# Two turned outputs into finished PSUM banks, and the last half's late sums, exponential and merge moved into block 7's first two quads

## The chip, the cores and the metric

The kernel runs on one core of one Trainium2 chip. The metric is the device time of one execution in microseconds (us). "A ratio" is fast runs of one kernel over fast runs of another, of the same rounds on the same chip. It is not quite the ratio of the medians quoted beside it.

Engines are named as in the profile: PE (the tensor engine, matmuls), DVE (VectorE), ACT (ScalarE), POOL (GpSimd). L382 is a line of the kernel.

## The reference

```python
def setup_inputs():
    m, k, n = 1024, 4096, 4096
    return {"a": randn(m, k), "b": randn(k, n)}      # float32

def reference(a, b):
    x = np.matmul(a, b)
    return special.logsumexp(x, axis=-1).astype(np.float32)
```

The 1024 x 4096 product is never stored. Its eight column blocks of 512 are reduced, one by one, to a maximum and a sum of exponentials per row, and these are merged at the end.

## The kernel before

The kernel computes most blocks with a two-by-two scheme of seven products (m1 to m7) instead of eight; VectorE makes the sums of operands that this needs (`t1`, `t3`, `t4`, `t6`, `t7`). It takes 16 matmuls for a product. Blocks 3 to 6 are "wide": each is done in two halves, whose outputs come out transposed. They are *turned* in 32 x 32 squares, and then reduced. Block 7 is done in four "quads" of seven products. After it come a reloaded block 0 and a reloaded block 1 for the last quarter of the rows.

How a wide half turns its four outputs and what it leaves for later:

```python
    def lse_turned(c, slot, h, r, by_rows=False):
        nm = tnm[:, 1 + h, ts(r, WN // 2)]
        v = blocks32(slot)
        nc.vector.transpose(out=slot, in_=c)
        nc.vector.tensor_reduce(out=nm, in_=v, axis=AX.X, op=ALU.max, negate=True)
        # ... (by_rows: 16 exponentials of 32 columns on ScalarE)
        add(v, v, nm.unsqueeze(-1).broadcast_to((P, WN // 2, 32)))
        nc.scalar.activation(out=slot, in_=slot, func=AF.Exp)
        return lambda: nc.vector.tensor_reduce(
            out=tts[:, 1 + h, ts(r, WN // 2)], in_=v, axis=AX.X, op=ALU.add
        )

    # end of wide_step; "last" is the last half before the narrow block 7
            end12 = lse_turned(c12, slots[0], 1, 0)
            end22 = lse_turned(c22, slots[1], 1, 1, True)
            product(c21, ...)                       # m4
            sub(s[:, 1], c21, s[:, 1])
            end12()
            end21 = lse_turned(c21, slots[0], 0, 1)
            end22()
            # t4, t7: all of them, or in the last half quarters 0 and 1
            product(c11, ...)                       # m7
            add(c11, c11, s[:, 1])
            e = fix_pool.tile([P, FD], f32, ..., tag="e")
            end11 = lse_turned(c11, e, 0, 0)
            end21()
            if last:
                # t4 and t7 of block 7, quarters 2 and 3: T4's upper half is where the slots lie
            deferred.extend([end11, merge_turned])
```

`deferred` runs in the next half or quad right after its first two sums; `pending` runs (by `flush`) just before these sums. `merge_turned` is a chain DVE, POOL, ACT, POOL on small tiles. The narrow quad, cut to the order of issue, which is each engine's order of execution:

```python
            m1(c11, start=True); m5(c12)
            nc.scalar.copy(out=e, in_=halves(r0))         # e = s[:, 0:2]
            m2(c21, start=True); m6(c22)
            nc.scalar.copy(out=s[:, 2], in_=c21)
            flush()
            if early and q == MP - 1:                     # block 7, fourth quad
                for g in range(G - 1):
                    last.make("t1", g * GI, (g + 1) * GI) # needs the load into aT
            add(s[:, 2], s[:, 2], e[:, 1])
            sub(s[:, 0], s[:, 2], e[:, 0])
            for f in deferred: f()
            # ... (more sums for the next blocks)
            m3(c12); nc.scalar.copy(out=x[:, 0], in_=c12) # x = s[:, 1::2]: over e[:, 1]
            m4(c21); nc.scalar.copy(out=x[:, 1], in_=c21)
            m7(c11)
            # ... (sums, then maxima; their exponentials go to pending)
            if early and q == 1:                          # block 7, second quad
                for what in ("t1", "t6", "t3"):
                    nxt.make(what)                        # 12 f16 sums on VectorE
            # ...
            if early and q == 1:
                spread_turned()                           # 32 small copies on GpSimd
                last = again1().load_all()                # 4 loads of b into aT, by GpSimd
```

## Time and profile before

| | before |
|---|---|
| median time | 421.74 us (421.0 to 422.65, 6 runs) |
| span of the profiled execution | 419.6 us |
| PE busy | 411.4 us, 98% |
| one wide half | 24.17 us |
| block 7's quads 1, 2, 3, 4 | 14.39, 12.22, 12.23, 12.23 us |
| reloaded block 0's quad | 12.22 us |

A quad's length is taken from the start of its first product to the start of the next one's. From the page: the first line gives each engine's busy time, share of the span and instructions, the second the clock that PE was granted, in tenths, in 40 slices of the span.

```profile
PE 411.4 (98%) x2747; PEld 260.9 (62%) x2747; DVE 316.5 (75%) x709; ACT 120.9 (29%) x447; POOL 92.0 (22%) x189
...
PEclk9999999999999999999999999999999999999999
```

So PE is the limit, and what can be won is the time in which it stands. The timeline of PE shows where (columns: start, duration, engine, line, operation, output and inputs, shape, count; in brackets the idle time before it and what ended it). The lines are the first quad's m1, m3, m4, m7, and the m1 of the second quad:

```profile
339.94 1.91 PE L554 MATMUL acc_0_0_3277<-tb,s_71 128*128 128x256 f16 x16
...
347.93 0.60 PE L554 MATMUL acc_0_0_3277<-b_0_2891,aT 128*128 128x256 f16 x4 [0.83 <-ACT s_0_3279 L621]
...
349.67 1.91 PE L554 MATMUL acc_0_1_3278<-tb,aT 128*128 128x256 f16 x16
352.58 0.60 PE L554 MATMUL acc_0_0_3277<-b_0_2891,aT 128*128 128x256 f16 x4 [1.00 <-ACT s_0_3279 L696]
...
354.33 1.91 PE L554 MATMUL acc_1_0_3411<-tb,s_71 128*128 128x256 f16 x16
```

The two brackets, 0.83 and 1.00 us by the profile's modelled ends, make a quad of 14.39 us instead of 12.22 (by the starts, against the second quad's, m3 came 1.0 us late and m7 2.16). In the timeline of ACT the copies that PE waited for (L621, L696) stand behind two exponentials that waited for others (L391 for c11 turned, L405 in the merge):

```profile
346.77 0.63 ACT L391 ACTIVATE ew_1_3259<-ew_1_3259 128x512 f32<-128x512 f32 x1 [3.01 <-DVE ew_1_3259 L86]
347.31 0.57 ACT L621 COPY s_0_3279<-acc_0_0_3277 128x512 f32<-128x512 f32 x1
...
351.99 0.28 ACT L405 ACTIVATE ident<-ident 128x96 f32<-128x96 f32 x1 [3.84 <-POOL ident L399]
352.18 0.35 ACT L696 COPY s_0_3279<-acc_0_0_3277 128x256 f32<-128x256 f32 x1
```

VectorE was late for the first; the merge, reached only when VectorE had done its sums, held up the second. GpSimd's timeline has the first and last of the 32 spread copies, which follow the merge, and the four loads into aT. The loads had to wait for the second quad's last product anyway:

```profile
353.94 0.19 POOL L415 COPY negmax<-ident 32x8 f32<-32x8 f32 x1
...
359.52 0.20 POOL L415 COPY tsum<-tts 32x8 f32<-32x8 f32 x1
366.00 3.56 POOL L149 DMA_DIRECT2D aT<-in_b_dram  x4 [6.28 <-PE acc_1_0_3411 L554]
```

### The profile page before, as it was taken

How to read it: one execution, taken by the hardware profiler on the slowest of the kernel's cores; microseconds unless marked ns; L12 is line 12 of the kernel's file. 1: busy time of each engine (PE TensorE's matmuls, PEld its weight loads, DVE VectorE, ACT ScalarE, POOL GpSimd, SP SyncE). 2: the span in 40 equal slices, each digit the busy share in tenths (PEclk: the TensorE clock that was granted, in tenths of full speed). 3: DMA queues.
4: the chain of work that ended last, by engine and by line, in shares of the span. 5: the costliest groups of instructions: out<-in, count | busy, mean ns of one | idle time of the engine just before them, and what ended most of it. 6: DMA issues, size and time to landing. Idle time of an engine off the chain costs nothing.

```text
span 419.6 us, 7085 instructions
## 1 busy us (share of the span) xinstructions
PE 411.4 (98%) x2747; PEld 260.9 (62%) x2747; DVE 316.5 (75%) x709; ACT 120.9 (29%) x447; POOL 92.0 (22%) x189
## 2 busy tenths in 40 slices
PE   8999999999999999999999999999999998999996
PEld 3555558888888844444444444444444477888885
DVE  2566587978656648969787896978789997299955
ACT  2222250141132210605134060514215052222124
POOL 8677743001010120013101031013100234320000
PEclk9999999999999999999999999999999999999999
DMA  9999999999999399004970099102990079499000
GB/s 186 201 202 203 203 205 207 207 207 214 178 200 185 54 186 207 9 2 75 207 121 0 2 165 207 29 1 35 207 160 2 0 120 207 76 186 208 10 2 0
DMA packets 57841, 53.28 MB, mean 127 GB/s; under 512 B 10192, under 2 KB 56912, under 8 KB 57808
## 3 DMA queue, kind: packets, MB, share of 16 engines
q0 software_dynamic: 48928, 49.95, 72.1%
q1 hardware_dynamic: 8880, 2.89, 4.3%
q8 instruction: 21, 0.34, 0.3%
q14 instruction: 12, 0.10, 0.1%
HBM read 100.66 MB, written 2.10 MB: 245 GB/s over the span
## 4 chain that ended last, share of the span: by engine, by line
PE 91%; DVE 4%; DMA 3%; issue 1%; ACT 0%; POOL 0%; SPq 0%; DVEq 0%; ACTq 0%; POOLq 0%
PE acc_1_0_1347 L554 2%; PE acc_1_0_767 L554 2%; PE acc_2_0_769 L554 2%; PE acc_2_0_3587 L554 2%; PE acc_0_0_765 L554 2%; PE acc_1_0_3411 L554 2%; PE acc_3_0_3723 L554 2%; PE acc_3_0_1615 L554 2%; PE acc_2_0_1482 L554 2%; PE acc_0_0_1215 L554 2%; PE acc_3_0_3859 L554 2%; PE wide_1_1_3085 L441 2%; PE wide_0_0_2899 L441 2%; PE wide_1_1_2707 L441 2%; PE wide_0_2_2523 L441 2%; PE wide_1_0_2328 L441 2%
## 5 line engine op out<-in xcount | busy, mean ns | idle before, releaser
L554 PEld LDWEIGHTS <-aT 128*128 128x128 f16 x832 | 81.3, 98 | 11.8 <-issue 2.2
L441 PEld LDWEIGHTS <-tb 128*128 128x128 f16 x384 | 37.6, 98 | 45.1
L382 ACT ACTIVATE tb<-tb,ident 128x32 f32<-128x32 f32 x128 | 39.1, 306 | 6.6 <-DVE ident L379 6.6
L391 ACT ACTIVATE tb<-tb 128x512 f32<-128x512 f32 x16 | 9.9, 622 | 89.6 <-DVE tb L86 89.6
L399 POOL TENSOR_TENSOR ident<-ident,tmin 128x96 f32<-128x96 f32 x8 | 3.1, 385 | 131.7 <-DVE tmin L401 131.7
L205 POOL DMA_DIRECT2D tb<-in_a_dram x47 | 25.6, 549 | 5.8 <-issue 1.9
L234 PEld LDWEIGHTS <-aT 128*128 128x128 f16 x192 | 16.6, 98 | 14.1 <-DVE aT L227 1.4
L229 ACT COPY aT<-tps_100 128x512 f16<-128x512 f16 x24 | 14.1, 586 | 38.5 <-PE tps_100 L216 38.5
L227 DVE COPY aT<-tps_99 128x512 f16<-128x512 f16 x24 | 10.2, 424 | 19.3 <-PE tps_99 L216 19.3
L382 ACT ACTIVATION_READ_ACCUMULATOR tb<-tb,ident 128x1 f32 x128 | 23.8, 186 | 0.0
L216 PEld LDWEIGHTS <-tb 128*128 128x128 f16 x192 | 14.8, 100 | 13.3 <-DMA tb<-in_a_dram 2.8
L554 PEld LDWEIGHTS <-s_71 128*128 128x128 f16 x208 | 20.4, 98 | 2.8
L554 PEld LDWEIGHTS <-s_73 128*128 128x128 f16 x208 | 20.4, 98 | 2.3
L554 PEld LDWEIGHTS <-s_72 128*128 128x128 f16 x208 | 20.4, 98 | 2.3
L379 DVE TENSOR_REDUCE ident<-tb 128x16 f32<-128x512 f32 x24 | 16.5, 686 | 1.4
L89 DVE TENSOR_TENSOR aT<-aT 128x256 f16<-128x256 f16 (+1 forms) x56 | 16.1, 339 | 0.0
L86 DVE TENSOR_TENSOR tb<-tb,ident 128x512 f32<-128x512 f32 x16 | 11.1, 692 | 0.6
L392 DVE TENSOR_REDUCE tts<-tb 128x16 f32<-128x512 f32 x16 | 10.8, 677 | 0.0
L216 PE MATMUL tps_99<-ident,tb 128*128 128x128 f16 x96 | 9.5, 223 | 0.6 <-DMA tb<-in_a_dram 0.4
L86 DVE TENSOR_TENSOR s_71<-aT 128x256 f16<-128x256 f16 (+1 forms) x26 | 8.1, 313 | 2.5 <-ACT aT L229 2.1
L216 PE MATMUL tps_100<-ident,tb 128*128 128x128 f16 x96 | 9.5, 222 | 0.0
L86 DVE TENSOR_TENSOR s_73<-aT 128x256 f16<-128x256 f16 (+1 forms) x26 | 8.1, 313 | 0.0
(907 smaller groups left out, 939.9 us busy)
## 6 DMA issues: line engine op xcount, KB each, us to landing
tb<-in_a_dram POOLq DMA_DIRECT2D x47, 128.0 KB, 5.9
aT<-in_b_dram POOLq DMA_DIRECT2D x4, 1024.0 KB, 15.1
b_1_86<-in_b_dram POOLq DMA_DIRECT2D x4, 256.0 KB, 6.4
b_2_87<-in_b_dram POOLq DMA_DIRECT2D x4, 256.0 KB, 6.2
b_3_88<-in_b_dram POOLq DMA_DIRECT2D x4, 256.0 KB, 6.2
b_0_89<-in_b_dram POOLq DMA_DIRECT2D x2, 512.0 KB, 9.3
b_1_90<-in_b_dram POOLq DMA_DIRECT2D x2, 512.0 KB, 12.5
b_2_91<-in_b_dram POOLq DMA_DIRECT2D x2, 512.0 KB, 15.9
```

The costliest lines, as they stand in the source:

```text
L86: nc.vector.tensor_tensor(out=o, in0=x, in1=y, op=ALU.add)
L89: nc.vector.tensor_tensor(out=o, in0=x, in1=y, op=ALU.subtract)
L205: nc.gpsimd.dma_start(out=slot, in_=a_m[m, :, k0 * P : (k0 + kn) * P])
L216: nc.tensor.matmul(pst[:, ts(j, P)], src[:, ts(j, P)], ident, is_transpose=True, start=(j == 0), stop=(j == kn - 1),)
L227: nc.vector.tensor_copy(out=dst, in_=v)
L229: nc.scalar.copy(out=dst, in_=v)
L234: nc.tensor.matmul(pt, aT[:, i, kp, m // 2, m % 2, :], blk0.raw[i // GI][:, i % GI, kp, :], start=(done[m] == 0), stop=(done[m] == KT - 1),)
L379: nc.vector.tensor_reduce(out=nm, in_=v, axis=AX.X, op=ALU.max, negate=True)
L382: nc.scalar.activation(out=v[:, i], in_=v[:, i], func=AF.Exp, bias=nm[:, i : i + 1], accum_out=tts[:, 1 + h, r * WN // 2 + i : r * WN // 2 ...
L392: return lambda: nc.vector.tensor_reduce(out=tts[:, 1 + h, ts(r, WN // 2)], in_=v, axis=AX.X, op=ALU.add)
L441: nc.tensor.matmul(c.rearrange("p (q m) -> p q m", m=P), lhs(i), rhs(i), start=(start and i == 0), stop=(stop and i == KP - 1), skip_group ...
L554: nc.tensor.matmul(c, lhs(i), rhs(i), start=(start and i == 0), stop=(i == KP - 1), skip_group_check=True,)
```

## The change

The intent: turn c21 into c22's PSUM bank and c11 into c12's, products that are finished and turned by then. The slots, which lie in T4's upper half, are then free earlier. In the last half, the late T4 and T7 sums, c21's sum and c11's exponential go behind the first quad's copies and sums; c11's sum and the merge go on to the second quad (through `pending`).

```diff
-            end21 = lse_turned(c21, slots[0], 0, 1)
+            end21 = lse_turned(c21, c22, 0, 1)
...
-            e = fix_pool.tile([P, FD], f32, name=f"ew_{blk.nb}_{nt}", tag="e")
-            end11 = lse_turned(c11, e, 0, 0)
-            end21()
+            exp11, end11 = lse_turned(c11, c12, 0, 0, late=True)
             if last:
                 for what in ("t4", "t7"):
                     for g in range(G // 2, G):
-                        mk(what, g * GI, (g + 1) * GI)
-            deferred.extend([end11, merge_turned])
+                        deferred.append(lambda w=what, g=g: nxt.make(w, g * GI, (g + 1) * GI))
+                deferred.extend([end21, exp11])
+                deferred.append(lambda: pending.extend([end11, merge_turned]))
+            else:
+                exp11()
+                deferred.extend([end21, end11, merge_turned])
```

(`lse_turned` returns the exponential and the sum apart when `late` is set.)

More of the change, by code (lines that the diff above doesn't have):

```diff
@@ L373, with lse_turned @@
     blocks32 = lambda t: t.rearrange("p (c n) -> p c n", n=32)
-    def lse_turned(c, slot, h, r, by_rows=False):
+    def lse_turned(c, slot, h, r, by_rows=False, late=False):
         nm = tnm[:, 1 + h, ts(r, WN // 2)]
@@ L390, in lse_turned @@
         add(v, v, nm.unsqueeze(-1).broadcast_to((P, WN // 2, 32)))
-        nc.scalar.activation(out=slot, in_=slot, func=AF.Exp)
-        return lambda: nc.vector.tensor_reduce(
+        exp = lambda: nc.scalar.activation(out=slot, in_=slot, func=AF.Exp)
+        total = lambda: nc.vector.tensor_reduce(
             out=tts[:, 1 + h, ts(r, WN // 2)], in_=v, axis=AX.X, op=ALU.add
         )
+        if late:
+            return exp, total
+        exp()
+        return total
     def merge_turned():
```

## The prediction

> **What bounds the kernel.** The tensor engine: by the page 411.4 of 419.6 us busy at full granted clock, and 91% of the chain of waits. In the timeline the wide halves follow each other every 24.17 us with no PE gap, and the quads after block 7's first take 12.2 us each. After the start-up (62 us, which the change leaves alone) there is one hole: block 7's first quad runs from 339.94 to 354.33 us, 14.39 against 12.22. So 2.17 us (0.5%) is all the change can win.
>
> **Why the hole is there** (timeline, chain). VectorE is late; it idles 0.4 us between 327 and 351 us. The last wide half ends on it with c11's add, turn, reduce, add (until 346.66), then c21's sum, four late makes of T4 and T7 (347.37 to 349.78), and only then the quad's two sums, c11's sum and the merge. ScalarE, in order, holds back the quad's copies twice:
> - c11's exponential waits 3.0 us for VectorE until 346.77, so the copy of c11|c12 starts at 347.31 and m3 about 1 us late (347.93);
> - the merge's exponential waits 3.84 us until 351.99, so the copy of m3's result starts at 352.18 and m7 about 1.2 us late (352.58).
>
> **What the change does.** It removes no work: the same VectorE operations of 0.6 to 0.75 us and exponentials of 0.62 us, two outputs turned into PSUM instead of SBUF. That empties the slots, which share T4's upper half, so the late makes need not wait for c21's sum. In the last half the late makes, c21's sum and c11's exponential move behind the quad's copies and sums; c11's sum and the merge move into the second quad.
>
> The Trainium skill ("Perfetto Trace Analysis", Optimizing Scalar/DVE Operations) puts VectorE's access overhead at about 60 ns on SBUF, 125 ns on PSUM. The trace shows no such difference: maxima read from PSUM take 0.68 us and follow every 0.60, like reductions in SBUF. My estimate is 0 to 0.5 us per half, inside the 4 us that VectorE idles (20.2 busy of 24.2).
>
> **The quad re-timed**, with the second quad's offsets: first copy at 343.8 us; m2/m6's copy 347.1; VectorE sums 347.5 to 348.3; makes at 348.3, 348.9, 349.5, 350.1, done 350.8. m3 starts on time at 346.95; m4 at 348.70, needing T4's third quarter at 349.57 (ready 349.0) and fourth at 350.0 (349.6); m7 at 350.45, needing its last quarter at 351.75 (350.8). c11's exponential fits in at 347.5. All waits vanish, with 0.4 to 0.5 us of slack; the second quad starts near 352.2.
>
> **Given back later?** The merge's exponential now sits behind the second quad's copy (about 359.6), so GpSimd's spread and the load into aT go out near 367 us instead of 366.0, with the PE 2.2 us ahead. The last quarter's sums then wait some 3 us on VectorE, which idles 4 us before the final quad. I expect no PE loss.
>
> **Predicted:** 421.74 - 2.1 = 419.6 us, 8 in 10 within 418.8 to 420.9. Faster by over 2%: 0.005; within 2%: 0.985; slower: 0.01.
>
> **Would show it right:** no PE wait on ScalarE in block 7's first quad, its length near 12.2; wide halves still 24.17; VectorE durations on PSUM unchanged; the aT load about 1 us later; the tail unchanged.
>
> **Would make it wrong:** slower PSUM targets, making VectorE late for m4 or m7; m4 waiting for all of T4 instead of quarters (about 1 us lost); the later load reaching the final quads.

## More of the kernel before

Note for later: the copy into `x[:, 0]` overwrites `e[:, 1]`, so it has to wait until VectorE has read it; m7 waits for that copy; and the tile `s` has one buffer, shared by all quads.

One more place matters later, the fourth quad. In VectorE's timeline the three T1 sums that need the load (tb from aT) stand ahead of the quad's first sum (s_3_3725):

```profile
383.77 1.89 DVE L86 TENSOR_TENSOR tb<-aT 128x1024 f16<-128x1024 f16 x3
386.37 0.43 DVE L86 TENSOR_TENSOR s_3_3725<-s_3_3725 128x256 f32<-128x256 f32 x1 [0.72 <-ACT s_3_3725 L625]
```

Here that sum waits for ACT, by 0.72 us, and not for the load.

## The result, and the profile after

| | before | after |
|---|---|---|
| median time | 421.68 us (20 runs) | 425.84 us (425.58 to 426.42, 10 runs) |
| ratio | | 1.0102 (95%: 1.0091 to 1.0112) |
| span of the profiled execution | 419.6 us | 423.1 us |
| block 7's quads 1, 2, 3, 4 | 14.39, 12.22, 12.23, 12.23 | 12.23, 12.23, 12.22, 18.09 us |
| reloaded block 0's quad | 12.22 | 12.22 us |
| loads into aT issued, before the fourth quad's start | 12.78 us | 5.58 us |

The kernel became 1% slower. The 2.16 us of the first quad were won exactly as forecast, and 5.86 us were lost in the fourth. The page:

```profile
PE 411.8 (97%) x2747; PEld 260.9 (62%) x2747; DVE 315.6 (75%) x709; ACT 120.5 (28%) x447; POOL 96.2 (23%) x189
...
PEclk9999999999999999999999999999999999999899
```

PE's timeline, first quad (m1, m3, m4, m7, and the next m1, cut off after 11 of its 16 matmuls by the end of the window asked for): no bracket is left.

```profile
339.65 1.91 PE L560 MATMUL acc_0_0_3263<-tb,s_71 128*128 128x256 f16 x16
...
346.64 0.60 PE L560 MATMUL acc_0_0_3263<-b_0_2884,aT 128*128 128x256 f16 x4
...
348.38 1.91 PE L560 MATMUL acc_0_1_3264<-tb,aT 128*128 128x256 f16 x16
350.13 0.60 PE L560 MATMUL acc_0_0_3263<-b_0_2884,aT 128*128 128x256 f16 x4
...
351.88 1.36 PE L560 MATMUL acc_1_0_3395<-tb,s_71 128*128 128x256 f16 x11
```

PE's timeline, the fourth quad's m7 (the first and last of four groups of four matmuls; then the next quad's m1):

```profile
391.28 1.01 PE L560 MATMUL acc_3_0_3715<-b_0_2884,aT 128*128 128x256 f16 x4 [4.30 <-ACT s_3_3717 L702]
...
393.80 0.79 PE L560 MATMUL acc_3_0_3715<-b_3_2887,aT 128*128 128x256 f16 x4
394.42 1.91 PE L560 MATMUL acc_3_0_3851<-s_71 128*128 128x256 f16 x16
```

m7 should have begun 10.48 us after its quad, as in the first quad, at 386.81. It began at 391.28, 4.47 us late; and its 16 matmuls then took 3.14 us (391.28 to 394.42) instead of 1.75, which is 1.39 us more. Together that is the 5.86 us. The bracket names ACT's copy into x (L702). ACT in turn had waited for VectorE. Its timeline, the merge's exponential and this copy:

```profile
359.06 0.37 ACT L631 COPY s_1_3397<-acc_1_1_3396 128x256 f32<-128x256 f32 x1 [2.86 <-PE acc_1_1_3396 L560]
359.33 0.29 ACT L409 ACTIVATE ident<-ident 128x96 f32<-128x96 f32 x1
...
390.86 0.37 ACT L702 COPY s_3_3717<-acc_3_0_3715 128x256 f32<-128x256 f32 x1 [5.62 <-DVE s_3_3717 L86]
```

And VectorE had waited for the load: three T1 sums, then the quad's first sum that the copy needs.

```profile
381.33 0.68 DVE L86 TENSOR_TENSOR tb<-aT 128x1024 f16<-128x1024 f16 x1
384.71 0.69 DVE L86 TENSOR_TENSOR tb<-aT 128x1024 f16<-128x1024 f16 x1 [2.70 <-DMA aT<-in_b_dram]
389.74 0.69 DVE L86 TENSOR_TENSOR tb<-aT 128x1024 f16<-128x1024 f16 x1 [4.34 <-DMA aT<-in_b_dram]
390.35 0.42 DVE L86 TENSOR_TENSOR s_3_3717<-s_3_3717 128x256 f32<-128x256 f32 x1
```

GpSimd's timeline says why the load was late: the merge's second step waited 4.61 us for ACT, whose exponential stood behind a copy of the second quad; then the 32 copies, of which the first take 0.19 us (but for one of 0.69) and the last eight some 0.6; and then the loads, with no wait of their own.

```profile
359.70 0.44 POOL L403 TENSOR_TENSOR tts<-tts,ident 128x96 f32<-128x96 f32 x1 [4.61 <-ACT ident L409]
...
361.08 0.19 POOL L419 COPY negmax<-ident 32x8 f32<-32x8 f32 x1
...
365.69 0.19 POOL L419 COPY tsum<-tts 32x8 f32<-32x8 f32 x1
365.93 0.65 POOL L419 COPY negmax<-ident 32x8 f32<-32x8 f32 x1
366.52 0.66 POOL L419 COPY tsum<-tts 32x8 f32<-32x8 f32 x1
...
370.14 0.67 POOL L419 COPY tsum<-tts 32x8 f32<-32x8 f32 x1
370.75 3.57 POOL L149 DMA_DIRECT2D aT<-in_b_dram  x4
```

The granted clock in the stretch of m7, with the busy time of the engines (the columns are named by the first line):

```profile
core 0: us, PE busy (x) PEld busy (x) DVE busy (x) ACT busy (x) POOL busy (x), PEclk, DMA share, GB/s
391.20:394.50 3.30, 3.22 (x17) 2.29 (x17) 1.83 (x4) 0.30 (x2) 0.00 (x0) 0.55 0.84 142
```

### The profile page after: what moved, and what is told of

It reads as the page before. It is cut to its first block, busy times and chain, and to the rows that moved or that the text cites. A ratio compares the mean times of both kernels' runs of the same rounds, so it can differ in the third digit from the quotient of the medians.

```text
span 423.1 us, 7100 instructions
## 1 busy us (share of the span) xinstructions
PE 411.8 (97%) x2747; PEld 260.9 (62%) x2747; DVE 315.6 (75%) x709; ACT 120.5 (28%) x447; POOL 96.2 (23%) x189
## 4 chain that ended last, share of the span: by engine, by line
PE 86%; DMA 8%; POOL 3%; issue 1%; DVE 0%; ACT 0%; POOLq 0%; ACTq 0%; DVEq 0%
DMA aT<-in_b_dram 4%; DMA tb<-in_a_dram 3%; PE acc_1_0_1347 L560 2%; PE acc_1_0_767 L560 2%; PE acc_2_0_769 L560 2%; PE acc_3_0_3851 L560 2%; PE acc_0_0_3263 L560 2%; PE acc_3_0_1615 L560 2%; PE acc_2_0_1482 L560 2%; PE acc_0_0_1215 L560 2%; PE acc_0_0_765 L560 2%; PE wide_1_2_3078 L445 2%; PE wide_0_0_2892 L445 2%; PE wide_1_1_2701 L445 2%; PE wide_0_2_2518 L445 2%; PE wide_1_0_2324 L445 2%
## 5 line engine op out<-in xcount | busy, mean ns | idle before, releaser
L391 ACT ACTIVATE tb<-tb 128x512 f32<-128x512 f32 x8 | 5.0, 630 | 90.1 <-DVE tb L86 90.1
L379 DVE TENSOR_REDUCE ident<-tb 128x16 f32<-128x512 f32 x16 | 11.0, 686 | 1.1
L86 DVE TENSOR_TENSOR tb<-aT 128x1024 f16<-128x1024 f16 x8 | 5.2, 687 | 8.7 <-DMA aT<-in_b_dram 8.7
L86 DVE TENSOR_TENSOR s_71<-aT 128x256 f16<-128x256 f16 (+1 forms) x26 | 8.2, 314 | 2.4 <-ACT aT L229 1.5
L86 DVE TENSOR_TENSOR s_72<-aT 128x256 f16<-128x256 f16 (+1 forms) x26 | 8.2, 314 | 0.0
L86 DVE TENSOR_TENSOR s_73<-aT 128x256 f16<-128x256 f16 (+1 forms) x26 | 8.1, 313 | 0.0
```

The source lines that it names most:

```text
L86: nc.vector.tensor_tensor(out=o, in0=x, in1=y, op=ALU.add)
L391: exp = lambda: nc.scalar.activation(out=slot, in_=slot, func=AF.Exp)
```

## The experiments

My theory after the result: the merge and the spread delay the load into aT; VectorE's order then turns the late load into a wait of PE; and the wait brings a slow clock. The rivals: the PSUM targets cost the time; or the load is late for a reason of its own; or only the order of VectorE's work is at fault, not the lateness. The profile already spoke against the first (wide halves of 24.17 us, the same turning times), but only an experiment can say what each part costs by itself. All experiments but one gave a correct result.

| run | chip | this, us | before, us | ratio (95%) | load's lead, us | quads 1, 4, next |
|---|---|---|---|---|---|---|
| e1 loads first | 5 | 419.54 | 421.46 | 0.9952 (0.9940 to 0.9964) | 12.78 | 12.23, 12.23, 12.22 |
| e2 before, loads first | 5 | 421.52 | 421.46 | 0.9999 (0.9987 to 1.0011) | 12.78 | 14.40, 12.22, 12.23 |
| e3 merge after quad 1 | 5 | 419.39 | 421.46 | 0.9946 (0.9934 to 0.9958) | 12.78 | 12.23, 12.23, 12.22 |
| e4 sums first | 5 | 424.63 | 421.46 | 1.0094 (1.0070 to 1.0118) | 5.58 | 12.23, 12.23, 17.45 |
| e5 PSUM only | 1 | 421.22 | 421.24 | 1.0004 (0.9992 to 1.0016) | 12.78 | 14.18, 12.23, 12.22 |
| e6 late, SBUF, loads first | 1 | 419.39 | 421.24 | 0.9961 (0.9949 to 0.9973) | 12.78 | 12.64, 12.23, 12.22 |
| e7 filler | 1 | 424.67 | 421.24 | 1.0088 (1.0075 to 1.0102) | 5.59 | 12.23, 16.66, 12.98 |
| e8 no sums (wrong result) | 1 | 421.00 | 421.24 | 1.0007 (0.9986 to 1.0029) | 9.03 | 12.22, 13.26, 12.99 |
| e9 24 copies first | 12 | 420.02 | 421.54 | 0.9957 (0.9941 to 0.9972) | 10.51 | 12.23, 12.23, 12.62 |
| e10 both mends | 12 | 419.28 | 421.54 | 0.9942 (0.9928 to 0.9956) | 12.78 | 12.23, 12.22, 12.23 |
| e11 after again | 14 | 425.83 | 421.48 | 1.0103 (1.0086 to 1.0119) | 5.58 | 12.23, 18.01, 12.66 |

"Lead" is the start of the fourth quad less the start of the first load's issue; "next" is the reloaded block 0's quad.

### e1: the loads ahead of the spread

```diff
             if early and q == 1:
-                spread_turned()
                 last = again1().load_all()
+                spread_turned()
```

> The changed kernel with the four loads into aT put ahead of the 32 spread copies on GpSimd. Theory (the load goes out 4.8 us late because it stands behind the copies): load issued at about 364 us, when the second quad's last product ends, no wait in block 7's fourth quad (12.2 us instead of 18.1), no slow clock after it; 419.5 us, 2.2 below the kernel before. The 32 copies now run under VectorE's f16 sums and take about 0.6 us each, harmless. Rival (the PSUM targets or the moved VectorE work cost the time, and the load only shows it): stays near 425.8.

Measured: 419.54 us. The loads went out at 363.54 us, the fourth quad took 12.23 us, and PE's only waits are in the start-up. GpSimd's timeline, the loads and the first of the copies behind them:

```profile
363.54 3.57 POOL L149 DMA_DIRECT2D aT<-in_b_dram  x4 [2.54 <-PE acc L560]
367.07 0.70 POOL L419 COPY negmax<-ident 32x8 f32<-32x8 f32 x1
```

The whole loss came from the load's place behind the copies. The rival that PSUM or the moved VectorE work costs the time is out. The copies behind the load are as slow as expected, and harm nothing, since only the last merge reads what they write.

### e2: the same swap in the kernel before

```diff
             if early and q == 1:
-                spread_turned()
                 last = again1().load_all()
+                spread_turned()
```

> The kernel before with the same swap (loads ahead of the spread). There GpSimd already waited 6.3 us for the second quad's products before the load, so the load cannot go out earlier than 366.0: theory says same, 421.7 within 0.3. If the swap is a gain by itself, 419 to 421.

Measured: 421.52 us, ratio 0.9999. The swap is no gain by itself; it only takes away what the change brought in.

### e3: the merge at the end of the first quad

```diff
-                deferred.append(lambda: pending.extend([end11, merge_turned]))
+                deferred.append(lambda: after_quad.extend([end11, merge_turned]))
...
                 maxima()
+            for f in after_quad:
+                f()
+            after_quad.clear()
```

> The changed kernel with c11's sum and the merge issued at the end of block 7's first quad, ahead of the second quad's copies on ScalarE, and the load still behind the spread. Theory (the merge's exponential stood 4.6 us behind a copy, which pushed the spread under VectorE's f16 sums): merge's exponential near 355.1, copies of 0.19 us done by about 362.5, load issued near 364.0, fourth quad 12.2 us; 419.5 us. Rival (the spread is slow or late whatever the merge does): fourth quad still over 15 us, 423 or more.

Measured: 419.39 us. GpSimd's merge step now waits 0.40 us for ACT, where it waited 4.61, and the loads go out at 364.16 with all the copies done before, at 0.19 us for most and 0.29 at most:

```profile
356.11 0.38 POOL L404 TENSOR_TENSOR tts<-tts,ident 128x96 f32<-128x96 f32 x1 [0.40 <-ACT ident L410]
...
357.37 0.19 POOL L420 COPY negmax<-ident 32x8 f32<-32x8 f32 x1
...
364.16 3.57 POOL L149 DMA_DIRECT2D aT<-in_b_dram  x4 [0.78 <-PE acc L561]
```

So the merge's place on ACT is the root. Late by 4.6 us, it pushed the last copies under VectorE's sums, and these pushed the load.

### e4: the fourth quad's sums ahead of the load-dependent ones

```diff
-            if early and q == MP - 1:
-                for g in range(G - 1):
-                    last.make("t1", g * GI, (g + 1) * GI)
             add(s[:, 2], s[:, 2], e[:, 1])
             sub(s[:, 0], s[:, 2], e[:, 0])
+            if early and q == MP - 1:
+                for g in range(G - 1):
+                    last.make("t1", g * GI, (g + 1) * GI)
```

> The changed kernel with the fourth quad's two sums put ahead of the three T1 sums that wait for the load. Theory (the load's lateness itself costs, since VectorE's work that depends on it has to be done before the next quad's sums): the wait leaves the fourth quad, but one of 3 to 5 us on ScalarE's copy comes in the next quad (the reloaded block 0), since its sums stand behind eight f16 sums that now start near 396 us; 423.5 to 426.5. Rival (only the order of these sums behind the load-dependent ones costs, VectorE has slack to absorb the rest): no wait anywhere, 419.5.

Measured: 424.63 us. The fourth quad took 12.23 us, and the next one 17.45. ACT's timeline has its first copy, PE's the m3 that waited for it:

```profile
397.95 0.59 ACT L627 COPY s<-acc 128x512 f32<-128x512 f32 x1 [10.14 <-DVE acc L86]
```

```profile
398.58 3.02 PE L560 MATMUL acc<-b,aT 128*128 128x256 f16 x16 [2.45 <-ACT s L627]
401.39 2.51 PE L560 MATMUL acc<-s,aT 128*128 128x256 f16 x16
404.68 1.91 PE L560 MATMUL acc<-b,aT 128*128 128x256 f16 x16 [0.78 <-ACT s L702]
```

Total as expected, place as expected, cause of the larger wait not: I had named the next quad's sums. The copy into `e` waited 10.14 us for VectorE's adds into the fourth quad's outputs, which come behind the load-dependent sums. It fits that the tile `s` has one buffer, so that the next quad cannot fill it before the last one's readers are done. The sums that I had named account for the smaller wait, 0.78 us before m7. The rest of this quad's loss is the clock: m3 took 2.81 us instead of 1.75, and the granted clock was at half from 399.2 to 402.6 us. The order on VectorE decides where the late load hurts; it does not remove the loss.

### e5: PSUM targets alone

```diff
-            end21 = lse_turned(c21, slots[0], 0, 1)
+            end21 = lse_turned(c21, c22, 0, 1)
...
-            e = fix_pool.tile([P, FD], f32, name=f"ew_{blk.nb}_{nt}", tag="e")
-            end11 = lse_turned(c11, e, 0, 0)
+            end11 = lse_turned(c11, c12, 0, 0)
```

> The kernel before with only the two targets of the turning moved into PSUM (c21 into c22, c11 into c12), no order changed. Theory (PSUM targets cost and bring nothing by themselves): 421.7 within 0.4, hole of the first quad still 2.2 us, wide halves 24.17 us, turning and sums 0.6 to 0.75 us each as on SBUF. Rival (PSUM targets are slower on VectorE by tens of ns per operation): VectorE later by 0.2 to 0.5 us at the end of the last half, hole longer by as much, 422 or more.

Measured: 421.22 us, ratio 1.0004: neither cost nor gain that these runs can tell. The first quad's hole is still there, 14.18 us against 14.39.

### e6: the moved order with SBUF targets

```diff
-            end21 = lse_turned(c21, c22, 0, 1)
+            end21 = lse_turned(c21, slots[0], 0, 1)
...
-            exp11, end11 = lse_turned(c11, c12, 0, 0, late=True)
+            e = fix_pool.tile([P, FD], f32, name=f"ew_{blk.nb}_{nt}", tag="e")
+            exp11, end11 = lse_turned(c11, e, 0, 0, late=True)
             if last:
+                deferred.append(end21)
...
-                deferred.extend([end21, exp11])
+                deferred.extend([exp11])
```

(and the loads ahead of the spread, as in e1)

> The changed kernel with the loads ahead of the spread and both outputs turned into SBUF as before; c21's sum must then come before the late makes, 0.6 us later for T4's third quarter (near 349.6 us, with m4 needing it at about 349.6). Theory (the moved order closes the hole, PSUM only frees the slots so that the makes need not wait): first quad 12.2 to 12.8 us; 419.5 to 420.1. If the PSUM targets carry the gain: the hole stays near 2 us, 421.5.

Measured: 419.39 us, ratio 0.9961, within the noise of e1's 0.9952. The first quad took 12.64 us instead of 12.23; its m4 (349.46 to m7's start at 351.61) took 2.15 us instead of 1.75. So the moved order closes the hole, and the PSUM targets add the last 0.4 us by the trace; the times cannot tell them apart.

### e7: filler in the wait

```diff
+            if early and q == MP - 1:
+                dummy = psum_pool.tile([P, FD], f32, name="dummy", tag="ps")[:, 0:H]
+                for i in range(36):
+                    nc.tensor.matmul(dummy, s1[:, i % KP, q], aT[:, i % KP, 0, q], start=True, stop=True)
             m7(c11)
```

> The changed kernel with 36 idle-filling products (128 x 256, results unused) ahead of the fourth quad's last product, where the tensor engine waits some 4.3 us. Theory (16 products after the wait took 3.30 us instead of 1.75 because the engine had stood idle): the wait shrinks to about 0.4 us, the 16 products take 1.75 us, the time falls by 1.5 us to about 424.3; the load is as late as before. Rival (the products are slow because of what VectorE or the transfers do at that time): still 3.3 us, 425.8 or more.

PE's timeline: the filler, the shortened wait, m7, and the next m1.

```profile
386.88 4.09 PE L708 MATMUL dummy<-aT,s 128*128 128x256 f16 x36
391.31 1.91 PE L560 MATMUL acc<-b,aT 128*128 128x256 f16 x16 [0.34 <-ACT s L702]
393.06 1.91 PE L560 MATMUL acc<-s 128*128 128x256 f16 x16
```

m7 took 1.75 us again (391.31 to 393.06), with VectorE and the transfers as late as before (m7 4.43 us behind its place). The granted clock, asked in windows of 0.1 us, stayed at 1.00 through both quads. The slow matmuls were thus due to PE standing idle, and 1.39 us of the fourth quad's loss were the clock. The time fell by less than the expected 1.5 us, since the next quad, starting earlier, now met the late VectorE and took 12.98 us instead of 12.22. The net over the two quads is 0.67 us. The ratio went from 1.0102 to 1.0088, but the two intervals overlap, so the gain in time is shown by the trace alone.

### e8: the changed kernel without the twelve sums (wrong on purpose)

```diff
-            if early and q == 1:
-                for what in ("t1", "t6", "t3"):
-                    nxt.make(what)
```

> The changed kernel without the twelve f16 sums that VectorE makes for the reloaded block 0 after the second quad (result wrong on purpose). Theory (the spread copies on GpSimd take 0.6 instead of 0.19 us because VectorE's f16 sums run at the same time): all 32 copies near 0.19 us, load issued near 367 us instead of 370.8, wait in the fourth quad 0 to 1 us, 419.5 to 420.5. Rival (late copies because of the merge's late exponential alone, copies slow for another cause): eight copies still 0.6 us, load after 370, 425 or more.

The last copies on GpSimd now take 0.20 us, and the load goes out 9.03 us before the fourth quad instead of 5.58:

```profile
368.09 0.20 POOL L419 COPY tsum<-tts 32x8 f32<-32x8 f32 x1
368.23 3.57 POOL L149 DMA_DIRECT2D aT<-in_b_dram  x4
```

The late copies are slow because VectorE's sums run beside them: that accounts for 9.03 - 5.58 = 3.45 us of the 7.20 us by which the load's lead shrank, and the merge's place for the other 3.75. One of the 32 copies still took 0.70 us, as in the changed kernel; there it began at 363.01, when a VectorE subtraction (two SBUF inputs) had begun at 362.96. The fourth quad lost 1.03 us and the next 0.77. The time, 421.00 us, is above the expected 419.5 to 420.5, because I had left out the loss in the next quad.

### e9: 24 copies, then the loads, then eight copies

```diff
             if early and q == 1:
-                spread_turned()
+                spread_turned(range(3))
                 last = again1().load_all()
+                spread_turned(range(3, 4))
```

(`spread_turned` takes the groups as an argument.)

> The changed kernel with 24 of the 32 spread copies ahead of the loads into aT and the eight that ran slowly behind them. Theory (the loss is set by how long before the fourth quad the load goes out: 5.6 us in the changed kernel gave 4.5 us of wait in it, 9.0 us without the twelve sums gave 1.0 there and 0.8 in the next): load issued near 366 us, 10.4 us before the fourth quad; no loss in the fourth quad, 0.2 to 0.6 us in the next; 419.5 to 420.1, at most 0.6 above the version with all copies behind. Rival (any load behind the merge loses time): 421 or more.

Measured: 420.02 us; a lead of 10.51 us, no loss in the fourth quad, 0.40 us in the next. With e8 and the changed kernel this gives three points of loss against lead: 10.51 us costs 0.40, 9.03 costs 1.80, 5.58 costs 5.86 with the slow clock. For the fourth quad one number fits all three. In the changed kernel the lead shrank by 7.20 us and m7 came 4.47 late, so 2.73 us were to spare. In e8 it shrank by 3.75, which leaves 1.02, and the quad lost 1.03; in e9 by 2.27, which leaves nothing, and nothing was lost. So e8's missing sums did not distort its point there; for the next quad that was not tested.

### e10: both mends

The edits of e1 and e3 together.

> The changed kernel with both mends: merge at the end of the first quad, loads ahead of the spread. The load waits for the second quad's last product in either, so theory: no gain over one mend alone, 419.4 within 0.4. If a second hidden cost remained in one of them: below 419.

Measured: 419.28 us, ratio 0.9942. No gain over one mend alone that these runs can tell. It has the lowest median of the versions, though not by more than the noise, and it is the simplest one to defend, since neither the merge nor the spread is then in the load's way. Each of e1, e3, e6, e9 and e10 beats both kernels.

### e11: the changed kernel again

> The changed kernel once more, unedited: its first profile explains 3.4 us of loss, while the runs showed 4.2 and the profiled run was its fastest. Theory (the wait for the load varies between executions, since it follows transfers): a second profile shows the same two changes, the first quad 12.2 us and the fourth between 17.5 and 19.5, all other quads 12.2 us; median 425 to 426. Rival (a further loss elsewhere that the first profile did not have): another quad or a wide half longer by 0.5 us or more.

Measured: 425.83 us, ratio 1.0103. The second profile has the same two changes, and the fourth quad's wait is as long (m7 4.56 us behind its place). But the slow matmuls now reached into the next quad, which took 12.66 us; here m7 and that quad's m1:

```profile
393.18 3.19 PE L560 MATMUL acc<-b,aT 128*128 128x256 f16 x16 [4.39 <-ACT s L702]
396.15 2.34 PE L560 MATMUL acc<-s 128*128 128x256 f16 x16
```

No other quad is longer by 0.5 us. Over the two quads the loss was 6.22 us against 5.86 in the first profile. The theory's reason did not show itself: the wait was the same within 0.1 us. What varied is where the slow clock lay. Asked in windows of 0.1 us, the granted clock is at half for 3.41 us in both profiles (and in e4), but from 390.75 us in the first, 0.53 before m7 began, and from 393.61 in this one, 0.43 after m7 began, so that more of it fell on work.

This does not explain why the usual loss (4.2 us, by the medians) is 0.7 us above that of the profiled spans (423.1 - 419.6 = 3.5 us): of the ten runs behind the median, nine have the mean clock of the first profile or 0.001 above it (0.994, 0.995), and only one has this one's 0.991. Some 0.3 us of it may be that block 7 began at 339.65 us in the first profile after and at 339.94 in the one before; the rest stays open (block 7 began anywhere from 339.3 to 341.5 us in the profiles of all runs, so the start-up alone moves single runs by more than that).

## Why the prediction was wrong

1. **The hole in the first quad.** Right: 14.39 us became 12.23, all the waits went, and the second quad began 12.23 us after the first. The offsets from the quad's start were right within 0.1 us (m3, m4 and m7 on time), but for the first copy, which waited for c11's sum on VectorE and came 0.7 us later than forecast (344.23); that cost nothing. With the loss taken away (e1, e3, e10) the median is 419.3 to 419.5 us, where the forecast said 419.6.
2. **PSUM as a target.** Right: e5 is the same as before. Turning into PSUM takes 0.72 to 0.73 us against 0.72 into SBUF, the sum in place 0.70 against 0.69.
3. **"I expect no PE loss."** This is the step that failed; it lost 5.86 us. The prediction had named "the later load reaching the final quads" as a thing that would make it wrong, but put no loss on it. The step had two mis-sized terms and one thing overlooked:
   - *The load near 367 us, about 1 us later than before.* It went out at 370.75, 4.75 us later. I saw the merge's exponential go behind the second quad's copy (forecast 359.6, measured 359.33), but took the 32 copies at the 0.19 us that they had in the profile before. There VectorE was idle or reading PSUM. Moved later, the last eight ran beside VectorE's f16 sums at 0.56 to 0.67 us. The Trainium skill has this in "SBUF — State Buffer", section "SBUF: two separate sides": VectorE and GpSimd share a pair of ports, by an exclusive lock for a whole instruction, and a VectorE operation with two SBUF inputs takes it against a GpSimd operation that reads SBUF. The trace agrees, and e8 shows it by experiment: without the sums the copies take 0.20 us.
   - *"The last quarter's sums then wait some 3 us on VectorE."* I looked only at the last quarter of the load. The first three quarters' T1 sums stand ahead of the fourth quad's own sums on VectorE; the copy into x needs these, and m7 needs the copy. That path had 2.73 us to spare (e9), and the load came 7.20 us nearer. Nor would the forecast time of the load have been harmless: e8's lead of 9.03 us, which is about a load at 367.3 on the changed kernel's clock (376.33 - 9.03), still cost 1.80 us. VectorE's 4 idle us before the final quad come too late to help: PE has lost its time by then.
   - *The clock.* I had no term for it. PE stood for 4.3 us, and the next 16 matmuls took 3.14 us instead of 1.75. The Trainium skill's "TensorE: Matmul & The Clock Gate" ("What's actually happening") says that PE falls to half its clock after an idle window of about 3.4 us. The trace agrees (the granted clock was 0.50 from 390.75 to 394.16 us, after a wait of 4.3 us; for a shorter wait see the last section), and e7, by filling the wait, took away the 1.39 us.
4. **The sum.** Predicted -2.1 + 0; measured -2.16 + 4.47 + 1.39 = +3.70 in the quads of the first profile, with the median of the runs at +4.2. The mechanism of the gain was right and of the right size; the term "given back later" was put at 0 and was 5.86.

Ruled out: a cost of PSUM (e5, to within 0.2%), a gain of the swapped loads as such (e2), and a fault of order alone (e4).

## What to carry to other kernels

When work is moved behind a later point on one engine, follow it on to the engines that it feeds until the next transfer is issued: here a merge put behind one copy brought the last of 32 tiny copies under VectorE's sums, and a load 7.2 us nearer to its use. Take a duration over only if its neighbours stay the same; here a GpSimd copy took 0.19 us beside an idle VectorE and about 0.6 beside its sums. And issue a load ahead of any work in its queue that nobody waits for.

## What the Trainium skill lacked or had wrong

- "TensorE: Matmul & The Clock Gate" ("What's actually happening") names an idle window of about 3.4 us before the clock falls. In e4 a shorter wait did it: by the bracket 2.45 us, by the start 2.61 us late, and the 16 matmuls after it took 2.81 us (398.58 to 401.39) instead of 1.75. The granted clock fell at 399.20 us, when PE had already been at work again for 0.62 us. Waits of 1.0 us by the bracket (first quad of the kernel before) did not do it.
- "SBUF — State Buffer" ("SBUF: two separate sides") has the lock but no figure for many small GpSimd operations beside a row of VectorE sums. Here a 32 x 8 copy of 0.19 us took 0.56 to 0.67 us beside f16 sums that repeat every 0.60, so that each copy cost about one sum. That is no rule: in e9 the first copy behind the loads took 4.11 us (370.07 to 374.18), about as long as the rest of VectorE's row of sums.
- "Perfetto Trace Analysis" ("Optimizing Scalar/DVE Operations") gives VectorE's access overhead as about 60 ns on SBUF and 125 ns on PSUM. The turned outputs do not show that difference: 0.72 to 0.73 us for the turning into either (it reads PSUM in both cases), and 0.70 us in PSUM against 0.69 in SBUF for the sum in place, which tests it better. The same section's lower figure for ScalarE on PSUM does fit: the exponential of 128 x 512 took 0.57 to 0.59 us in PSUM at the end of the changed kernel's last half, and 0.61 to 0.63 us in SBUF in the kernel before.
